# Keeping the first query gate's weights from the K projection on, with advance products of that gate alone

## The chip, the cores and the metric

The kernel runs as one program on one core of a Trainium2 chip. The metric is device time in microseconds (us). The engines are TensorE (PE: matmuls, with weight loads shown as PEld), VectorE (DVE), ScalarE (ACT), GpSimd (POOL) and SyncE (SP, which here only issues DMA transfers). Each engine works through its own queue in order; ACT's queue holds DMA issues too. SBUF is the on-chip memory, PSUM the memory into which PE adds up products.

## The reference

One layer of a transformer-like block over 1024 tokens of width 1024, in float32. What matters here is the first sub-layer:

```python
h = rmsnorm(x, ln1_g[l]) * (1.0 + sc1) + sh1
p = h @ w_in[l]
q, k, v, cb, cc, cx, ga, gb = jnp.split(p, split_at, axis=-1)
q = rmsnorm(q.reshape(b, s_len, SB_HEADS, SB_HEAD_DIM), q_norm_g[l])
k = rmsnorm(k.reshape(b, s_len, SB_HEADS, SB_HEAD_DIM), k_norm_g[l])
...
y_a = stick_breaking_attention(q, k, v)
y_b = cb * causal_dwconv(cc * cx, conv_w[l])
merged = (jax.nn.sigmoid(ga) * (y_a @ w_branch_a[l])
          + jax.nn.sigmoid(gb) * (y_b @ w_branch_b[l]))
x = x + g1 * (merged @ w_out[l])
```

After it come a second norm and a SwiGLU feed-forward part, which the change does not touch. All inputs are drawn at random; the norms' gains are scaled up (ln1_g by 2.738, q_norm_g and k_norm_g by 8).

## The kernel before

**Split numbers.** A float32 matrix is held as a high part and a low part (hi, lo), and a product is three matmuls: hi by hi, hi by lo, lo by hi. A weight tile `raw` (128 x 1024) comes from memory over SP. ACT writes its high part `whi` with a copy, and DVE the low part `wlo` with a subtraction. `g_split` (line 471) does so for half a tile, that is 128 x 512.

**Stages around the change.** The activations h are kept in SBUF, in four tiles named `big` (high and low part of two halves of the tokens). The K projection (from line 440) runs over two halves of the columns (`cc` 1 and 2) and eight blocks of 128 tokens (`i`); one block is 24 matmuls. Each block has a tail, `finish_k` (line 382): ACT squares the block (`qsq`), DVE sums per head (`qss`), POOL forms the reciprocal root (`rs_m`, `rs_r`), DVE scales (`qn`), PE transposes (four small matmuls into `tr`, line 396), ACT writes the high part `khl` (line 399), DVE its low part (line 400), and ACT issues two transfers to `d_k` (line 402). The transposes of a block come some blocks after it, so the last two stand behind the end of the projection.

While the K projection runs, a generator `factors` computes four combinations of the halves of h and writes them to memory as `d_t[6]`, `d_t[3]`, `d_t[5]`, `d_t[4]`, since SBUF has no room for them yet.

**The gates.** The other projections are computed as 20 "gates". Gate g makes two blocks of 128 output columns, j and j + 4, for all tokens. It is a Strassen-like scheme: the 2 x 2 blocks a11, a12 (tile `raw`) and a21, a22 (tile `raw2`) of the weights are combined on POOL to ws1 to ws4 (`s1` to `s4` in the code), and seven products are formed instead of eight. A product is 12 matmuls of 128 x 512 (`half_prod`, line 125) of one weight combination with one factor of h:

- p1: a11 with factor 0, and p2: a12 with factor 1; both factors lie in `big`
- p3: ws4 with factor 2, in `big` as well
- p4: a22 with factor 3, which is loaded from `d_t[3]` over a part of `big` that is free after the K projection (two transfers of 1 MB, line 632)
- p5: ws1 with factor 4, p6: ws2 with factor 5, p7: ws3 with factor 6; these are the tiles `ft`, of 2 MB each. `ft` 4 and 5 are loaded during the K projection (line 459), `ft` 6 after it (line 630), since its place is in a pool that opens only then

Gates 0 to 3 are the query gates (section 5, weights `w_q`). For them `put_q` writes q to memory and squares it, and `sum_q` adds up the squares with small matmuls (line 587) for the norm.

**Advance products.** Before the loop over gates, `first_two` loads `raw` of gates 0 and 1 and forms p1 and p2 of both (NG = 2): four products, in PSUM before the loop starts. Their loads and splits run during the K projection. In the loop, `two_raw` loads both weight tiles of a gate; it is called for gate g + 1 when POOL's work on gate g is issued. Two `raw` buffers exist (GR = 2). Gate 0's two tiles are loaded by a call of `two_raw(0)` ahead of the loop, so its `raw` is loaded twice, and gate 1's as well.

**Order.** The kernel is written in a tile language: a scheduler fixes each engine's order when the kernel is built, from the order of the program and a model of the time, and puts in the waits. `tc.issue_after(X)` keeps an instruction behind X in that order.

Of the kernel before, what the change touches and what calls it, by code (L numbers as in the profile page):

```python
# [8 lines left out]
F32 = mybir.dt.float32  # L9
F32R = mybir.dt.float32r  # L10
AF = mybir.ActivationFunctionType
ALU = mybir.AluOpType
# [4 lines left out]
P = 128  # L17
# [12 lines left out]
def block_kernel(tc, x, x_t, cols, ada_1, ada_2, ada_row, w_q, w_kv, w_v1, w_cg, w_a, w_b, w_o, w_g, w_u, w_d, out):  # L30
    nc = tc.nc
# [7 lines left out]
    def nm(s):  # L39
        uid[0] += 1  # L40
        return f"{s}_{uid[0]}"

    def big():
        return bigp.tile([P, KT, 512], F32R, tag="big", bufs=4, name=nm("big"))
# [9 lines left out]
    def load_w(src):  # L54

        wp, bufs = wps
        raw = gw.tile([P, 1024], F32, tag="raw", bufs=GR, name=nm("raw"))
        nc.sync.dma_start(raw, src)
        hi = wp.tile([P, 1024], F32R, tag="whi", bufs=bufs, name=nm("whi"))
        lo = wp.tile([P, 1024], F32R, tag="wlo", bufs=bufs, name=nm("wlo"))  # L60
        nc.scalar.activation(hi, raw, AF.Copy)
        nc.vector.tensor_tensor(out=lo, in0=raw, in1=hi.bitcast(F32), op=ALU.subtract)
        return hi, lo
# [15 lines left out]
    d_t = {q: drp.tile([P, 2, 4, 512], F32, name=f"d_t{q}") for q in (6, 3, 5, 4)}  # L79
# [46 lines left out]
    def half_prod(ps, w, fh, fl):  # L126

        wh = w[0].rearrange("p (k m) -> p k m", k=4)
        wl = w[1].rearrange("p (k m) -> p k m", k=4)
        for k in range(4):  # L130
            nc.tensor.matmul(ps, wh[:, k, :], fh[:, k, :], start=(k == 0), stop=False)  # L131
            nc.tensor.matmul(ps, wh[:, k, :], fl[:, k, :], start=False, stop=False)  # L132
            nc.tensor.matmul(ps, wl[:, k, :], fh[:, k, :], start=False, stop=(k == 3))  # L133

    def tt(eng, out, a, b, op):
        eng.tensor_tensor(out=out, in0=a, in1=b, op=op)  # L136
# [5 lines left out]
    def ps_pj():  # L142
        return pps.tile([P, 512], F32, tag="pj", bufs=6, name=nm("pj"))
# [6 lines left out]
    GR, NG, GS, GS2 = 2, 2, 4, 3  # L150
    gws = ExitStack()
    gw = gws.enter_context(tc.tile_pool(name="wpl", bufs=1, reuse_waits="tile"))
# [131 lines left out]
    def mm_tok(ps, i, w, k0, k1, parts=(0, 1, 2)):  # L284

        n, t0 = i // 4, (i % 4) * P
        for k in range(k0, k1):
            wh = w[k // 2][0][:, (k % 2) * 512:(k % 2) * 512 + 512]
            wl = w[k // 2][1][:, (k % 2) * 512:(k % 2) * 512 + 512]
            sh = hh[n][:, k, t0:t0 + P]  # L290
            sl = hl[n][:, k, t0:t0 + P]
            for q, (a, b) in enumerate(((sh, wh), (sh, wl), (sl, wh))):
                if q in parts:
                    nc.tensor.matmul(ps, a, b, start=(k == 0 and q == 0), stop=(k == KT - 1 and q == 2))  # L294
# [88 lines left out]
    def finish_k(ps, i, ch):  # L383
        sq = gw.tile([P, 512], F32, tag="wlo", bufs=GS, name=nm("qsq"))
        nc.scalar.activation(sq, ps, AF.Square)
        ss = ap.tile([P, 8], F32, tag="qss", bufs=3, name=nm("qss"))
        nc.vector.tensor_reduce(out=ss, in_=sq.rearrange("p (h d) -> p h d", d=DH), op=ALU.add, axis=AX.X)
        qn = ap.tile([P, 512], F32, tag="qn", bufs=2, name=nm("qn"))
        r = rstd_of(ss, 1.0 / DH, ap, 8)
        nc.vector.tensor_tensor(out=qn.rearrange("p (h d) -> p h d", d=DH),  # L390
                                in0=ps.rearrange("p (h d) -> p h d", d=DH),
                                in1=r.unsqueeze(2).broadcast_to([P, 8, DH]), op=ALU.mult)
        yield
        tr = ps_tr()
        for j in range(4):
            nc.tensor.transpose(tr[:, j * P:(j + 1) * P], qn[:, j * P:(j + 1) * P], ident)
        hl_ = ap.tile([P, 2, 512], F32R, tag="vs", bufs=4, name=nm("khl"))
        hi, lo = hl_[:, 0], hl_[:, 1]
        nc.scalar.activation(hi, tr, AF.Identity, scale=kgc)
        nc.vector.scalar_tensor_tensor(out=lo, in0=tr, scalar=kgc, in1=hi.bitcast(F32), op0=ALU.mult, op1=ALU.subtract)  # L400
        for e, t in ((0, hi), (1, lo)):
            nc.scalar.dma_start(d_k[e][4 * ch:4 * ch + 4, :, i * P:(i + 1) * P].rearrange("j p t -> p j t"),
                                t.rearrange("p (j t) -> p j t", j=4).bitcast(F32))
# [9 lines left out]
    tails = []  # L413
# [19 lines left out]
    def more():  # L433

        with tc.issue_after(ends[0]), tc.issue_after(ends[1]):
            next(ml, None)

    for cc in (1, 2):
        w = wq[4:] if cc == 1 else [load_w(w_kv[cc, j]) for j in range(4)]
        for i in range(8):  # L440
            ps = ps_pj()
            mm_tok(ps, i, w, 0, 8)
            while len(tails) >= 2:
                next(tails.pop(0), None)
            tails.append(finish_k(ps, i, cc - 1))
            next(tails[-1])
            for _ in range(2 if (cc, i) < (1, 4) else 3):
                more()
            if (cc, i) == (2, 1):
                for _ in ml:  # L450
                    pass
                s2b.close()
                sx.close()
# [3 lines left out]
    ft = {q: ftp.tile([P, 2, 4, 512], F32R, name=f"ft{q}") for q in (5, 4)}  # L457
# [3 lines left out]
    def g_bank():  # L461
        return ps_pj()

    def g_raw(src):
        raw = gw.tile([P, 1024], F32, tag="raw", bufs=GR, name=nm("raw"))
        last_raw[0] = nc.sync.dma_start(raw, src)
        return raw

    last_raw = [None]

    split_at = [gw]

    def g_split(src):
        split_at.append(split_at.pop(0))
        hi, lo = (split_at[0].tile([P, 512], F32R, tag=t_, bufs=GS if split_at[0] is gw else GS2, name=nm(t_))
                  for t_ in ("whi", "wlo"))
        nc.scalar.activation(hi, src, AF.Copy)  # L477
        tt(nc.vector, lo, src, hi.bitcast(F32), ALU.subtract)
        return hi, lo

    fac = {0: (hh[0][:, 0:4], hl[0][:, 0:4]), 1: (hh[0][:, 4:8], hl[0][:, 4:8]), 2: (hh[1][:, 4:8], hl[1][:, 4:8])}
    def g_prod(w, q):
        ps = g_bank()
        half_prod(ps, w, *fac[q])
        return ps

    gates = ([(5, j) for j in range(4)] + [(sec, j) for j in range(4) for sec in (1, 2)] +
             [(sec, j) for sec in (4, 3) for j in range(4)])

    def w_of(sec, m):  # L490
        return w_q[m] if sec == 5 else w_cg[sec, m]

    pre = {}

    def first_two(g):
        sec, j = gates[g]
        raw = g_raw(w_of(sec, j))
        return g_prod(g_split(raw[:, :512]), 0), g_prod(g_split(raw[:, 512:]), 1)

    for g in range(NG):  # L500
        pre[g] = first_two(g)
        if g == 0:
            for tl in tails:
                next(tl, None)

    def two_raw(g):
        sec, j = gates[g]
        return g_raw(w_of(sec, j)), g_raw(w_of(sec, j + 4))

    s2.close()  # L510
    sw.close()
# [78 lines left out]
    def end_q():  # L590

        ss = [g_tile()[:H] for n in range(2)]
        for n in range(2):
            nc.scalar.activation(ss[n], ssq[n], AF.Copy)
        yield
        tr = g_bank()
        for i in range(8):
            nc.tensor.transpose(tr[:, i * H:(i + 1) * H], ss[i // 4][:, i % 4 * P:(i % 4 + 1) * P], ident[:H, :H])
        ms = gp.tile([P, 8, H], F32, name="ms16")
        nc.vector.tensor_scalar(out=ms.rearrange("p i h -> p (i h)"), in0=tr[:, :8 * H], scalar1=1.0 / DH, scalar2=EPS,  # L600
                                op0=ALU.mult, op1=ALU.add)
        for i in range(8):
            for h in range(0, H, 8):
                yield
                nc.gpsimd.tensor_tensor(out=rq[:, 0, i, h:h + 8], in0=ms[:, i, h:h + 8], in1=nhalf, op=ALU.pow)
        nc.vector.tensor_scalar(out=rq[:, 1], in0=rq[:, 0], scalar1=-1.0, scalar2=None, op0=ALU.mult)
# [18 lines left out]
        nc.scalar.dma_start(d_y[m, :, s:s + 512], y)  # L625

    uc = {}
    raws = two_raw(0)
    pend, pmm, eq = [], [], end_q()
    nc.sync.dma_start(ft[6].bitcast(F32), d_t[6])  # L630
    for e in range(2):
        nc.sync.dma_start(fac[3][e].bitcast(F32), d_t[3][:, e])
    for g, (sec, j) in enumerate(gates):
        raw, raw2 = raws
        p1, p2 = pre[g] if g in pre else (g_prod(g_split(raw[:, :512]), 0), g_prod(g_split(raw[:, 512:]), 1))
# [6 lines left out]
        if g + 1 < len(gates):  # L642
            raws = two_raw(g + 1)
# [374 lines left out]
    for n in range(2):  # L1018
        for k in range(KT):
            yr = fp.tile([P, 512], F32, tag="yr", bufs=2, name=nm("yr"))  # L1020
            nc.sync.dma_start(yr, d_ya[n][:, k, :])
            tag, bufs = slots[n * KT + k]
# [134 lines left out]
    tails, pre = [], {}  # L1157
    for ch in range(2):
        w = [] if ch else list(w_pre)
        for j in range(len(w) // 2, 4):  # L1160
            raw = load_raw(w_o[ch, j])
# [89 lines left out]
    th, tl = big(), big()  # L1251
# [335 lines left out]
```

## Time and profile before

| what | us |
|---|---|
| median of 3 runs | 1845.73 |
| lowest and highest run | 1843.6, 1846.24 |
| the profiled execution, its own time | 1843.09 |
| span of the profiled execution | 1841.3 |
| mean granted PE clock, share of full speed | 0.997 |

The page gives the busy time of each engine, the chain of work that ended last, and groups of instructions. A row of the view in order of time reads: start, length (of a merged group), engine, line, operation, the tile written and the tiles read, and in brackets the idle time before it and what ended it. In a row of the windows view come the length, then for PE, PEld, DVE, ACT and POOL the busy time with the number of instructions, then the granted PE clock, the share of time for which the DMA engines were busy, and GB/s. The view of waits gives who waited for whom: total, times, longest. A matmul's shown length reaches past the start of the next, so its cost is the distance of starts.

### The profile page before, as it was taken

To read this page: it belongs to the slowest core of one execution; us is meant where nothing else is said; L and a number is where in the kernel's file an instruction comes from. 1 tells how busy PE (TensorE), PEld (TensorE's weight loads), DVE (VectorE), ACT (ScalarE), POOL (GpSimd) and SP (SyncE) were. 2 spreads that over 40 slices of the span, in tenths; PEclk is the share of its full clock that TensorE was granted. 3 is DMA by queue.
4 is the path that set the end of the run, shared out by engine and by line. 5 is a ranking of instruction groups with operands and counts; after the bars stand their busy time and mean duration, and the time that the engine had idled before them with its cause. 6 is when DMAs were issued, how large, how long until landed. Compare 5 with 4: busy or idle time off the path is not lost.

```text
span 1841.3 us, 24885 instructions
## 1 busy us (share of the span) xinstructions
PE 1804.7 (98%) x8829; PEld 1502.7 (82%) x8829; DVE 1350.0 (73%) x1948; ACT 792.0 (43%) x1494; POOL 370.3 (20%) x277
## 2 busy tenths in 40 slices
PE   7999999999999999999999999999999999999999
PEld 4787778888879988888888788877888888878887
DVE  6874776779874888888887644589977788644776
ACT  4352553333343656565665311663444344422321
POOL 1043327423240000000000000105543454200000
PEclk9999999999999999999999999999999999999999
DMA  9588452227748565678554635424533344299766
GB/s 394 192 318 291 166 189 86 81 75 253 277 162 253 152 193 172 186 230 272 158 141 136 208 126 206 138 93 159 206 137 142 133 172 172 103 335 339 280 231 220
DMA packets 147267, 358.01 MB, mean 194 GB/s; under 512 B 15480, under 2 KB 44480, under 8 KB 144968
## 3 DMA queue, kind: packets, MB, share of 16 engines
q1 hardware_dynamic: 101816, 289.12, 46.2%
q10 hardware_dynamic: 44320, 63.64, 9.9%
q0 software_dynamic: 1008, 3.67, 0.5%
q8 instruction: 70, 1.15, 0.3%
q14 instruction: 53, 0.43, 0.1%
HBM read 245.74 MB, written 110.66 MB: 194 GB/s over the span
## 4 chain that ended last, share of the span: by engine, by line
PE 73%; DVE 11%; DMA 9%; ACT 3%; issue 3%; POOL 1%; SPq 0%; ACTq 0%; DVEq 0%; POOLq 0%
PE e L132 6%; PE e L131 6%; PE e L133 6%; PE pj L131 5%; PE pj L133 5%; PE pj L132 5%; PE pj L294 5%; PE pj L880 4%; PE pj L881 4%; PE pj L882 4%; PE e L1414 3%; PE e L1416 3%; PE e L1415 3%; PE tr L807 3%; PE o L823 2%
## 5 line engine op out<-in xcount | busy, mean ns | idle before, releaser
L792 DVE TENSOR_TENSOR_SCAN pt<-pt,mk 128x128 f32<-128x128 f32 (+7 forms) x128 | 171.9, 1349 | 47.3 <-ACT pt L788 47.1
L788 ACT ACTIVATE pt<-z,rq 128x512 f32<-128x512 f32 (+3 forms) x192 | 107.1, 579 | 89.5 <-PE z L787 57.6
L131 PE MATMUL e<-big,whi 128*128 128x512 f32 x352 | 137.2, 390 | 2.2 <-ACT c L1314 2.2
L133 PE MATMUL e<-big,wlo 128*128 128x512 f32 x352 | 137.1, 389 | 0.0
L132 PE MATMUL e<-big,whi 128*128 128x512 f32 x352 | 137.0, 389 | 0.0
L122 POOL TENSOR_SCALAR rs_m<-ss 128x1 f32<-128x1 f32 x8 | 1.7, 211 | 653.7 <-ACT xn L1217 653.7
L136 DVE TENSOR_TENSOR c<-e,c 128x512 f32<-128x512 f32 x138 | 92.8, 686 | 54.6 <-PE e L133 53.7
L131 PE MATMUL pj<-big,whi 128*128 128x512 f32 x320 | 125.1, 391 | 0.8 <-DVE c L136 0.8
L132 PE MATMUL pj<-big,whi 128*128 128x512 f32 x320 | 124.7, 390 | 0.0
L133 PE MATMUL pj<-big,wlo 128*128 128x512 f32 x320 | 124.3, 390 | 0.0
L1414 PE MATMUL e<-whi,f 128*128 128x512 f32 (+1 forms) x319 | 121.7, 382 | 1.6 <-DMA f<-d_f 1.6
L1415 PE MATMUL e<-wlo,f 128*128 128x512 f32 (+1 forms) x319 | 121.8, 382 | 0.0
L1416 PE MATMUL e<-whi,f 128*128 128x512 f32 (+1 forms) x319 | 121.6, 382 | 0.0
L294 PE MATMUL pj<-whi,big 128*128 128x512 f32 x352 | 110.0, 398 | 4.0 <-ACT big L277 3.9
L136 DVE TENSOR_TENSOR wlo<-raw,whi 128x512 fp32r<-128x512 f32 x116 | 88.4, 766 | 33.9 <-ACT whi L477 33.8
L136 DVE TENSOR_TENSOR c<-pj,c 128x512 f32<-128x512 f32 x140 | 93.1, 681 | 27.5 <-PE pj L133 26.9
L136 POOL TENSOR_TENSOR ws<-raw,raw 128x512 f32<-128x512 f32 x40 | 57.2, 1429 | 273.6 <-DMA raw<-w_cg 129.0
L477 ACT ACTIVATE whi<-raw 128x512 fp32r<-128x512 f32 x116 | 72.6, 629 | 88.3 <-PE pj L132 37.7
L811 DVE TENSOR_TENSOR atl<-tr,ath 128x512 fp32r<-128x512 f32 (+1 forms) x192 | 99.5, 547 | 14.4 <-ACT ath L810 12.6
L132 PE MATMUL e<-rl,whi 128*128 128x512 f32 x264 | 103.5, 392 | 2.5 <-DVE rl L136 2.5
L810 ACT ACTIVATE ath<-tr 128x512 fp32r<-128x512 f32 (+1 forms) x192 | 86.8, 489 | 44.5 <-PE o L822 26.0
L807 PE MATMUL tr<-dm,pt 128*128 128x128 f32 x576 | 98.0, 274 | 6.2 <-DVE atl L811 5.6
(255 smaller groups left out, 5021.6 us busy)
## 6 DMA issues: line engine op xcount, KB each, us to landing
f<-d_f SPq DMA_DIRECT2D x77, 512.0 KB, 4.3
d_f<-fs SPq DMA_DIRECT2D x70, 512.0 KB, 3.2
raw<-w_cg SPq DMA_DIRECT2D x40, 512.0 KB, 4.3
raw<-w_u SPq DMA_DIRECT2D x26, 512.0 KB, 3.2
raw<-w_g SPq DMA_DIRECT2D x25, 512.0 KB, 3.5
ad<-ada ACTq DMA_DIRECT2D x19, 512.0 KB, 5.5
ada<-ada SPq DMA_DIRECT2D x8, 1024.0 KB, 9.9
d_t<-ts SPq DMA_DIRECT2D x16, 512.0 KB, 4.0
```

The costliest lines, as they stand in the source:

```text
L131: nc.tensor.matmul(ps, wh[:, k, :], fh[:, k, :], start=(k == 0), stop=False)
L132: nc.tensor.matmul(ps, wh[:, k, :], fl[:, k, :], start=False, stop=False)
L133: nc.tensor.matmul(ps, wl[:, k, :], fh[:, k, :], start=False, stop=(k == 3))
L136: eng.tensor_tensor(out=out, in0=a, in1=b, op=op)
L294: nc.tensor.matmul(ps, a, b, start=(k == 0 and q == 0), stop=(k == KT - 1 and q == 2))
L788: nc.scalar.activation(pt[:, off + s0:off + s0 + m], z[:, :m], AF.Sigmoid, scale=rq[:, 1, i, h:h + 1])
L792: nc.vector.tensor_tensor_scan(out=pt[:, rev], data0=pt[:, rev], data1=mk[:, rev], initial=1.0, op0=ALU.mult, op1=ALU.max)
L807: nc.tensor.transpose(tr[:, j * P:(j + 1) * P], pt[:, off + (b0 + j) * P:off + (b0 + j + 1) * P], ident)
L811: nc.vector.tensor_tensor(out=tl[:, :nb, c0:c0 + P], in0=src, in1=th[:, :nb, c0:c0 + P].bitcast(F32), op=ALU.subtract)
L1414: nc.tensor.matmul(o, sh, w[0][:, c], start=(j == 0), stop=False)
L1415: nc.tensor.matmul(o, sh, w[1][:, c], start=False, stop=False)
L1416: nc.tensor.matmul(o, sl, w[0][:, c], start=False, stop=(j == NJ - 1))
```

## The change

The weights of gate 0 (`raw` and `raw2`) are loaded in the K projection, at block 3 of its second half, into the two `raw` buffers, and stay there until the loop uses them. The two halves of `raw` are split at that place. After the projection p1 and p2 of gate 0 alone are formed in advance; gate 1's come in the loop, as for the later gates. The call `two_raw(0)` ahead of the loop is gone, and with it the second load of gate 0's `raw` and the separate load of gate 1's: two loads of 512 KB fewer. The loads of `ft` 6 and of the two halves of factor 3 are held behind gate 0's second weight load, and in this order behind each other. The functions `g_raw`, `g_split`, `w_of`, `two_raw` and the list `gates` move up unchanged.

```diff
     for cc in (1, 2):
         w = wq[4:] if cc == 1 else [load_w(w_kv[cc, j]) for j in range(4)]
         for i in range(8):
+            if (cc, i) == (2, 3):
+                raws = two_raw(0)
+                pre_w = g_split(raws[0][:, :512]), g_split(raws[0][:, 512:])
             ps = ps_pj()
             mm_tok(ps, i, w, 0, 8)
...
-    pre = {}
-
-    def first_two(g):
-        sec, j = gates[g]
-        raw = g_raw(w_of(sec, j))
-        return g_prod(g_split(raw[:, :512]), 0), g_prod(g_split(raw[:, 512:]), 1)
-
-    for g in range(NG):
-        pre[g] = first_two(g)
-        if g == 0:
-            for tl in tails:
-                next(tl, None)
...
+    pre = {0: (g_prod(pre_w[0], 0), g_prod(pre_w[1], 1))}
+    for tl in tails:
+        next(tl, None)
...
     uc = {}
-    raws = two_raw(0)
     pend, pmm, eq = [], [], end_q()
-    nc.sync.dma_start(ft[6].bitcast(F32), d_t[6])
+    with tc.issue_after(last_raw[0].ins):
+        ld = nc.sync.dma_start(ft[6].bitcast(F32), d_t[6])
     for e in range(2):
-        nc.sync.dma_start(fac[3][e].bitcast(F32), d_t[3][:, e])
+        with tc.issue_after(ld.ins):
+            ld = nc.sync.dma_start(fac[3][e].bitcast(F32), d_t[3][:, e])
     for g, (sec, j) in enumerate(gates):
         raw, raw2 = raws
```

More of the change, by code (lines that the diff above doesn't have):

```diff
@@ L436, in more, with g_raw, g_split, w_of @@
             next(ml, None)
+    def g_raw(src):
+        raw = gw.tile([P, 1024], F32, tag="raw", bufs=GR, name=nm("raw"))
+        last_raw[0] = nc.sync.dma_start(raw, src)
+        return raw
+    last_raw = [None]
+    split_at = [gw]
+    def g_split(src):
+        split_at.append(split_at.pop(0))
+        hi, lo = (split_at[0].tile([P, 512], F32R, tag=t_, bufs=GS if split_at[0] is gw else GS2, name=nm(t_))
+                  for t_ in ("whi", "wlo"))
+        nc.scalar.activation(hi, src, AF.Copy)
+        tt(nc.vector, lo, src, hi.bitcast(F32), ALU.subtract)
+        return hi, lo
+    gates = ([(5, j) for j in range(4)] + [(sec, j) for j in range(4) for sec in (1, 2)] +
+             [(sec, j) for sec in (4, 3) for j in range(4)])
+    def w_of(sec, m):
+        return w_q[m] if sec == 5 else w_cg[sec, m]
+    def two_raw(g):
+        sec, j = gates[g]
+        return g_raw(w_of(sec, j)), g_raw(w_of(sec, j + 4))
     for cc in (1, 2):
@@ L462, in g_bank @@
         return ps_pj()
[L464 to L479, printed above, removed]
     fac = {0: (hh[0][:, 0:4], hl[0][:, 0:4]), 1: (hh[0][:, 4:8], hl[0][:, 4:8]), 2: (hh[1][:, 4:8], hl[1][:, 4:8])}
@@ L485, in g_prod @@
         return ps
[L487 to L491, printed above, removed]
-    pre = {}
-    def first_two(g):
-        sec, j = gates[g]
-        raw = g_raw(w_of(sec, j))
-        return g_prod(g_split(raw[:, :512]), 0), g_prod(g_split(raw[:, 512:]), 1)
-    for g in range(NG):
-        pre[g] = first_two(g)
-        if g == 0:
-            for tl in tails:
-                next(tl, None)
-    def two_raw(g):
-        sec, j = gates[g]
-        return g_raw(w_of(sec, j)), g_raw(w_of(sec, j + 4))
+    pre = {0: (g_prod(pre_w[0], 0), g_prod(pre_w[1], 1))}
+    for tl in tails:
+        next(tl, None)
     s2.close()
```

## The prediction

> **What bounds the kernel now.** I read the page first: its share of busy time and the chain that ended last.
>
> ```profile
> span 1841.3 us, 24885 instructions
> PE 1804.7 (98%) x8829; PEld 1502.7 (82%) x8829; DVE 1350.0 (73%) x1948; ACT 792.0 (43%) x1494; POOL 370.3 (20%) x277
> PE 73%; DVE 11%; DMA 9%; ACT 3%; issue 3%; POOL 1%; SPq 0%; ACTq 0%; DVEq 0%; POOLq 0%
> ```
>
> TensorE (PE) is busy 98% of the span, so whatever does not open or close a gap on PE is worth nothing here. All 24 moved matmuls stay in the program, so the question is only which PE gaps lie where the change acts: between the end of the K projection and the third gate. Second view: who PE waited for between 80 and 300 us.
>
> ```profile
> PE pj L131 <- ACT whi L477: 2.3, 1, 2.3
> PE tr L587 <- ACT gt L579: 0.7, 1, 0.7
> PE tr L587 <- DVE gt L136: 0.3, 1, 0.3
> ```
>
> These three are all that can be won by closing waits: 2.3 + 0.7 + 0.3 = 3.3 us. The first is the join between the advance products and the loop over gates. The other two are sums for the q norm that wait for a square and its split. Third view: PE in order of time around that join.
>
> ```profile
> 166.88 0.48 PE L131 MATMUL pj<-big,whi 128*128 128x512 f32 x1
> ...
> 168.82 0.60 PE L396 MATMUL tr<-dm,qn 128*128 128x128 f32 x4
> 169.17 0.48 PE L133 MATMUL pj<-big,wlo 128*128 128x512 f32 x1
> ...
> 178.63 0.40 PE L133 MATMUL pj<-big,wlo 128*128 128x512 f32 x1
> 181.29 0.80 PE L131 MATMUL pj<-ft,whi 128*128 128x512 f32 x1 [2.27 <-ACT whi L477]
> 181.88 0.63 PE L132 MATMUL pj<-ft,whi 128*128 128x512 f32 x1
> ...
> 191.09 0.39 PE L131 MATMUL pj<-big,whi 128*128 128x512 f32 x1
> ...
> 196.31 0.39 PE L133 MATMUL pj<-big,wlo 128*128 128x512 f32 x1
> ```
>
> 166.88 is the first advance product. From 191.09 to 196.31 stand 24 matmuls, so one takes (196.31 - 191.09) / 23 = 0.227 us, and a product of 12 takes 2.72. A group of four transposes takes 169.17 - 168.82 = 0.35. After the gap, matmuls last 0.63 instead of 0.39. The windows view shows what that is:
>
> ```profile
> 181.30:184.70 3.40, 3.40 (x8) 2.70 (x9) 3.36 (x5) 1.49 (x3) 0.41 (x1) 0.52 0.93 286
> 1271.70:1275.10 3.40, 3.40 (x15) 2.80 (x16) 3.37 (x6) 2.02 (x4) 0.00 (x0) 1.00 1.04 405
> ```
>
> The third number from the end is the granted PE clock: 0.52 for the 3.4 us after this gap, in which 8 matmuls run. The same length at clock 1.00 holds 15. So the low clock costs another 7 x 0.227 = 1.6 us. The gap counted from matmul starts is 181.29 - 178.63 - 0.23 = 2.43.
>
> **The change part by part.** *Two loads fewer.* Before, the weights of the first query gate are fetched once for the advance products and again for the loop. Now both halves are fetched at the two places in SP's order where the two advance loads stood, and kept. 1 MB of traffic and two issues go. No PE wait named a load of these, so I take 0 for it. The lower bound is a gain of one landing, if it alone held the join:
>
> ```profile
> raw<-w_q SPq DMA_DIRECT2D x10, 512.0 KB, 5.2
> ```
>
> *Splits.* Four advance splits become two, and the second gate's two go into the loop, each on ACT and DVE: the same number of instructions on each engine. *SP's order.* The reload of gate 0 stood ahead of the 2 MB load ft6; now ft6 and the two 1 MB halves of factor 3 come first, then the second gate's weights. In the built kernel the order of instructions differs from that of before only between the second half of the K projection and the third gate (three pairs of DVE instructions aside, much later). After that all engines run the same order, so what is lost or won here is carried unchanged to the end.
>
> *The gap, the main term.* The 24 products of gate 1 leave the place where they covered ACT's work after the K projection. In the new PE order both last transpose groups stand behind the 24 products that are left: PE is through at 166.88 + 24 x 0.227 + 2 x 0.35 = 173.0. Then it waits for the split of ws2 on ACT, as before. What ACT does between the transposes and that split:
>
> ```profile
> 167.93 0.37 ACTq L402 DMA_DIRECT2D d_k<-khl  x1
> 169.45 0.69 ACT L399 ACTIVATE khl<-tr,cst 128x512 fp32r<-128x512 f32 x1 [1.56 <-PE tr L396]
> ...
> 177.92 1.15 ACTq L402 DMA_DIRECT2D d_k<-khl  x2
> 179.12 1.08 ACT L670 ACTIVATE c<-pj 128x512 f32<-128x512 f32 x2 [1.23 <-DVE uu L613]
> 180.09 1.67 ACT L477 ACTIVATE whi<-ws 128x512 fp32r<-128x512 f32 x3
> ```
> ```profile
> 177.92 0.75 DVE L400 SCALAR_TENSOR_TENSOR khl<-tr,cst,khl 128x512 fp32r<-128x512 f32 x1 [6.40 <-ACT khl L399]
> ```
>
> New ACT order: khl, khl, four d_k issues, one copy of c, split of ws1, split of ws2. A khl starts 169.45 - 168.82 = 0.63 after its transposes. The first group begins at 166.88 + 5.45 = 172.33, so khl starts at 172.96 and the second 0.64 later, ending at 174.29. The last d_k issue needs DVE's low part of the second, two DVE instructions of 0.75 after 173.65, so 175.15; with 0.37 for the issue, 175.5. One copy: 0.49 (half of 180.09 - 179.12), 176.0. Two splits at 1.67 / 3 = 0.56: PE starts at **177.1**. Applied to before, where one khl starts at 177.20 and two copies follow, the same steps give 181.2 against the 181.29 shown. The new gap is 177.1 - 173.0 = 4.1, against 2.43: **+1.7 us**. POOL is the other limit:
>
> ```profile
> 168.41 1.64 POOL L123 TENSOR_TENSOR rs_r<-rs_m,nhalf 128x8 f32<-128x8 f32 x1
> 176.61 1.28 POOL L136 TENSOR_TENSOR ws<-raw,raw 128x512 f32<-128x512 f32 x1 [6.57 <-DMA raw<-w_q]
> 177.85 1.28 POOL L136 TENSOR_TENSOR ws<-raw 128x512 f32<-128x512 f32 x1
> 179.10 1.26 POOL L136 TENSOR_TENSOR ws<-raw,ws 128x512 f32<-128x512 f32 x1
> ```
>
> Before, POOL waited 6.57 us for the reloaded weights. Now they are there, and ws1 and ws2 follow the last rs_r: 170.05 + 3 x 1.26 = 173.8. That wait is truly removed, but ACT's queue in front of the split ends later. If ACT's queue did not hold it, PE would start at 173.8 + 0.6 = 174.4, a gap of 1.4. Bounds of this term: from -1.0 (POOL's gap) to +1.7; I take ACT's, since it is in order and each step has its row.
>
> *The clock.* Two gaps of this kernel were not followed by a low clock:
>
> ```profile
> 1271.68 0.50 PE L131 MATMUL e<-big,whi 128*128 128x512 f32 x1 [2.18 <-ACT c L1314]
> ```
> ```profile
> 1627.24 0.47 PE L1414 MATMUL e<-whi,f 128*128 128x512 f32 x1 [1.64 <-DMA f<-d_f]
> ```
>
> A gap of 2.27 was, a gap of 2.18 was not. A gap of 4.1 is longer than any of these, so I take one low stretch, 1.6 us, in both kernels: 0. Bounds -1.6 and +1.6 (none, or two stretches).
> The Trainium skill (TensorE: Matmul & The Clock Gate, Part 1: The HAM clock gate) says that PE falls to half rate after an idle window of about 3.4 us and is released after a busy window of that length. The trace agrees with the length and rate of the low stretch, and not with the idle time, 2.27 us here. By that rule the old gap would cost no clock and the new one would, which is a rival below.
>
> *The sums for the q norm.* Their waits of 0.7 and 0.3 came when gate 1 began with its third product. Now two more products (5.4 us) stand ahead, and the sums among them. I take -0.8 of the 1.1, bounds 0 and -1.1.
>
> *Gate 1's loads, now on the path.* Its first product begins at 177.1 + 60 x 0.227 + 1.6 = 192.3. What comes before it on SP, and how long transfers took (transfers by kind with their median to landing; SP in order of time; whom SP's issue of ft6 waited for; landings of raw, then of d_k, shortest, median and longest; two windows with the share of the DMA engines second to last):
>
> ```profile
> ft<-d_t SPq DMA_DIRECT2D x3, 2048.0 KB, 8.8
> ...
> d_k<-khl ACTq DMA_DIRECT2D x32, 256.0 KB, 4.4
> big<-d_t SPq DMA_DIRECT2D x2, 1024.0 KB
> ```
> ```profile
> 175.52 0.33 SPq L630 DMA_DIRECT2D ft<-d_t  x1
> ```
> ```profile
> SPq L630 <- DMA d_k<-khl: 5.8, 1, 5.8
> ```
> ```profile
> DMA to landing us min/median/max: 3.2/4.2/10.2
> ```
> ```profile
> DMA to landing us min/median/max: 2.2/4.4/14.9
> ```
> ```profile
> 170.00:175.00 5.00, 5.00 (x24) 4.11 (x23) 1.35 (x2) 0.14 (x1) 0.04 (x1) 1.00 1.00 316
> 175.00:180.00 5.00, 4.02 (x20) 3.00 (x18) 0.77 (x3) 1.57 (x3) 3.39 (x3) 1.00 1.12 369
> ```
>
> ft6 now needs only the end of the K projection (166.6): with 8.8 it lands at 175.4 and is used at 177.1 + 24 x 0.227 + 1.6 = 184.2. In the built kernel the second half of factor 3 waits for the d_k landing that released ft6 at 175.52; with at most 8.8 it is there at 184.3, used at 189.6. Gate 1's first weights wait for the next d_k landing, about 177, and with 10.2 (the longest of a weight load) land at 187.2; with 1.3 for the split that leaves 3.8 us. The second need the split of gate 0's last quarter (ACT and DVE, to about 180.5), land by 190.7, and with POOL's 3.8 and a split are ready at 195.1 for PE's 197.8. All are covered by gate 0's 60 matmuls, so I take 0; the DMA engines are full (1.00, 1.12) in this stretch, so the upper bound is the second rival.
>
> **Sum.** 0 + 1.7 + 0 - 0.8 + 0 = +0.9 us. The profiled execution took 1843.09 us, 1.8 around its span of 1841.3, so it would take 1844.0. The median of the three runs, 1845.73, is 2.64 above it; I put the 0.9 on the median: **1846.6 us**.
>
> **The rivals.** *The join closes.* PE does not wait for ACT's queue: the gap is POOL's 1.4 (-1.0) or none (-2.4), without low clock (-1.6) and without the sums' waits (-0.8 to -1.1). That is -3.4 to -5.1, 1842.3 to 1840.6; I price it at 1841.5. For it speaks POOL's 6.57 us wait, which goes; against it, the four d_k issues and two khl that stand ahead of the split on ACT.
> *The clock.* The old gap usually costs no low clock and the new one always does: +1.7 + 1.6 - 0.8 = +2.5, 1848.2. For it, the 2.18 us gap at clock 1.00; against it, the 0.52 after 2.27. This is what the Trainium skill's rule (TensorE: Matmul & The Clock Gate, Part 1) would make of it.
> *Gate 1's weights land late* (the other side). PE, which before had gate 1's first two products done, stands at their start. It decides from a landing later than 191 for the first or 193 for the second load. If the latter takes 14.9 us, as the slowest d_k transfer did, it lands at 195.4, ws2's split is ready at 199.7, and PE stands 1.9 us, with 1.6 of low clock: 0.9 + 3.5 = +4.4, 1850.1. For it, full DMA engines and 4 MB queued ahead; against it, several us of slack at each step.
> *The change does nothing*: gap, clock and sums as before, 1845.7.
>
> **How the numbers follow.** Forecast 0.48, clock 0.12, does nothing 0.05, late weights 0.17, join closes 0.18. A difference of 0.2% is 3.7 us, about what a measurement of this kernel can tell from no change. Late weights are over it and so is most of the closed join (0.16 of 0.18, with 0.02 short of it); of the forecast I give 0.03 to slower and 0.01 to faster, for errors in the terms. Slower 0.20, faster 0.17, same 0.48 + 0.12 + 0.05 + 0.02 - 0.04 = 0.63. The range goes from 1841.8, inside the closed join, to 1850.4, just over the late weights.
>
> **What would show it.** Right: PE waits once at the join, 4 us, for ACT's whi; POOL's first ws follows rs_r without a DMA wait; khl twice, then four d_k issues, on ACT before it; 8 matmuls of 0.63 behind it; no wait of L587's successor above 0.3; gate 1's first product without a wait. Wrong: a gap under 2.5 us at the join (ACT's queue mis-timed), a PE wait for raw or ft in gates 0 to 2 (loads), or a time off by over 4 us with this stretch as forecast, which would put the cause where the order is unchanged.

## The result and the profile after

The changed kernel takes 1852.34 us (median of 7 runs, 1849.2 to 1857.84) where the kernel before takes 1843.6 in the same comparison (7 runs, 1839.81 to 1846.24): ratio 1.0041, 95% interval 1.0029 to 1.0053. By this ratio it is slower by about 7.6 us (the medians differ by 8.7). I had forecast 0.9 us more than before; my 1846.6 and its range up to 1850.4 were too low. The profiled execution took 1849.2 us; its page says:

```profile
span 1847.4 us, 24886 instructions
...
PE 1804.0 (98%) x8829; PEld 1504.5 (81%) x8829; DVE 1349.1 (73%) x1948; ACT 794.1 (43%) x1494; POOL 368.3 (20%) x277
...
PE 80%; DVE 10%; DMA 4%; issue 2%; ACT 2%; ACTq 0%; SPq 0%; POOL 0%; DVEq 0%; POOLq 0%
```

PE is as busy as before (1804.0 against 1804.7 us), so the 6.1 us that the span grew are time in which PE stood. Whom it waited for between 80 and 300 us is now one line (total, times, longest):

```profile
PE pj L131 <- ACT whi L451: 9.0, 1, 9.0
```

The two waits of the sums for the q norm are gone, and the wait at the join has grown from 2.3 to 9.0 us. PE in order of time at that place:

```profile
172.32 1.03 PE L396 MATMUL tr<-dm,qn 128*128 128x128 f32 x8
182.36 0.80 PE L131 MATMUL pj<-ft,whi 128*128 128x512 f32 x1 [9.01 <-ACT whi L451]
182.96 0.63 PE L132 MATMUL pj<-ft,whi 128*128 128x512 f32 x1
```

Both groups of transposes stand behind the 24 advance products, as forecast, and PE is free where I had it (172.32 + 2 x 0.35 = 173.0). But the first matmul of the next product comes at 182.36, not at 177.1. ACT in order of time shows what it did until then:

```profile
172.96 1.26 ACT L399 ACTIVATE khl<-tr,cst 128x512 fp32r<-128x512 f32 x2 [5.20 <-PE tr L396]
173.68 6.95 ACTq L402 DMA_DIRECT2D d_k<-khl  x4
180.67 0.60 ACT L665 ACTIVATE c<-pj 128x512 f32<-128x512 f32 x1 [6.45 <-issue]
181.17 1.66 ACT L451 ACTIVATE whi<-ws 128x512 fp32r<-128x512 f32 x3
```

This is the forecast order, khl, khl, four d_k issues, c, splits, and the khl start at the forecast 172.96. Yet the four issues, for which I had reckoned until 175.5, last until 180.63. The chain of waits (start, length, engine or queue, line) has them one by one:

```profile
174.25 2.08 ACTq L402
...
176.37 3.27 ACTq L402
...
179.68 0.94 ACTq L402
```

The first of the four took the usual 0.37, the other three 2.08, 3.27 and 0.94. From 174.25 on ACT computes nothing: it stands in the issue of a transfer, and the copy c and the splits that PE needs are queued behind. POOL had long been ready, right after its last rs_r and without a wait for weights:

```profile
169.88 1.30 POOL L136 TENSOR_TENSOR ws<-raw,raw 128x512 f32<-128x512 f32 x1
...
172.38 1.27 POOL L136 TENSOR_TENSOR ws<-raw,ws 128x512 f32<-128x512 f32 x1
```

What changed for the transfers is seen in SP's queue. After, in order of time:

```profile
166.58 0.32 SPq L624 DMA_DIRECT2D ft<-d_t  x1
166.95 13.95 SPq L627 DMA_DIRECT2D big<-d_t  x2
```

The second row merges two issues of 0.3 to 0.4 us each (shortest, median, longest in ns, start of the first and of the last):

```profile
L627 SPq DMA_DIRECT2D big<-d_t x2: 319/371/423, 167.0 to 180.6; - x2
```

And before, a row that I had passed over:

```profile
163.77 0.80 SPq L632 DMA_DIRECT2D big<-d_t  x2
```

Before, factor 3 (`big`, 2 x 1 MB) was fetched from 163.77 on, that is while the K projection still ran and not after it, and ft6 (2 MB) from 175.52. The change chains factor 3 behind ft6: ft6 goes out 9 us earlier and factor 3 later. Its first half follows at 166.95. These 3 MB now move up to 179.6, across the time in which ACT has to issue the last d_k writes (by the trace's DMA packets, 0.9 MB are left at the first of these). The second half of factor 3 goes out at 180.6, when the d_k issues are over.

How much of the 6.1 us lies here? I take the starts of the 600th and the 1200th matmul (154 and 293 us before: ahead of the join, and several gates behind it). Between them lie 139.63 us before and 144.47 after: **4.8 us**. Taken as distances of matmul starts over 0.23 each, this is the gap at the join with 9.05 against 2.44 (+6.6), the two waits for the sums, 0.5 and 0.9, which are gone (-1.4), the low stretch with 1.4 against 1.6 (-0.2), and another -0.2. The order of instructions behind is the same in both kernels. From the 1200th to the 1700th matmul all eleven profiles of this study take 113.3 us. The four stretches from there to the end (starts at 407, 543, 810 and 1195 us before) differ by 1.9 to 6.1 us among the eleven, and between the two runs of the changed kernel (this one and c1) by up to 1.6. The other 1.3 us of the two profiles lie there, and I don't explain them.

### The profile page after: what moved, and what is told of

Its sections match the earlier page's. It is cut to its first block, busy times and chain, and to the rows that moved or that the text cites. A ratio compares the mean times of both kernels' runs of the same rounds, so it can differ in the third digit from the quotient of the medians.

```text
span 1847.4 us, 24886 instructions
## 1 busy us (share of the span) xinstructions
PE 1804.0 (98%) x8829; PEld 1504.5 (81%) x8829; DVE 1349.1 (73%) x1948; ACT 794.1 (43%) x1494; POOL 368.3 (20%) x277
## 3 DMA queue, kind: packets, MB, share of 16 engines
q8 instruction: 70, 1.15, 0.3%
## 4 chain that ended last, share of the span: by engine, by line
PE 80%; DVE 10%; DMA 4%; issue 2%; ACT 2%; ACTq 0%; SPq 0%; POOL 0%; DVEq 0%; POOLq 0%
PE e L131 7%; PE e L132 7%; PE e L133 7%; PE pj L131 6%; PE pj L133 6%; PE pj L132 6%; PE pj L294 5%; PE pj L875 4%; PE e L1409 4%; PE e L1411 4%; PE e L1410 4%; PE pj L876 4%; PE pj L877 4%; PE tr L802 3%; PE o L818 2%
```

## The experiments

Theory (held issues): the d_k issues on ACT stand because data that was queued earlier is still moving, and everything behind them on ACT, and PE, stands with them. Rivals: one unlucky execution; ACT's queue is simply this long; the loads slow PE itself. Where a kernel was timed, the ratio is to the kernel before on the same chip.

**c1: the changed kernel once more**, with no edit.

> The changed kernel once more, as the control of this group. Its profile had a PE gap of 9.0 us at the join, of which ACT's four d_k issues took 6.95 us. Theory (held issues: the d_k issues on ACT stand while the 4 MB of factor loads fill the DMA engines): gap 8 to 10 us again, four issues 6 to 8 us, 7 to 9 us slower than before. Rival (one unlucky execution; the ordinary gap is the 4.1 us of ACT's short rows): gap 4 to 5 us here, issues under 2.5 us.

Ratio 1.0032 (1.0023 to 1.0042). PE waits 8.7 us at the join, and ACT in order of time shows the same picture:

```profile
173.78 6.67 ACTq L402 DMA_DIRECT2D d_k<-khl  x4
```

Not one unlucky execution.

**e1: both factor loads behind gate 1's first weights**, in gate 0, so that they are issued when ACT is past its d_k issues.

```diff
-    with tc.issue_after(last_raw[0].ins):
-        ld = nc.sync.dma_start(ft[6].bitcast(F32), d_t[6])
-    for e in range(2):
-        with tc.issue_after(ld.ins):
-            ld = nc.sync.dma_start(fac[3][e].bitcast(F32), d_t[3][:, e])
...
+        if g == 0:
+            n_sec, n_j = gates[1]
+            r1 = g_raw(w_of(n_sec, n_j))
+            with tc.issue_after(last_raw[0].ins):
+                ld = nc.sync.dma_start(ft[6].bitcast(F32), d_t[6])
...
+            with tc.issue_after(ld.ins):
+                raws = r1, g_raw(w_of(n_sec, n_j + 4))
```

> The same, with the loads of ft6 and of factor 3 behind the second gate's first weight load, so that they are issued at about 175 us, after the d_k issues. Held issues: the four d_k issues take under 2.5 us, the gap at the join is 4 to 5 us, and the time falls by 4 to 6 us against the changed kernel, unless factor 3 comes late for the fifth product (a PE wait for it, up to 4 us, would then eat it). Rival (the queue in front of the split is long by itself, the loads have no part): gap 9 us as in the changed kernel, no gain.

Ratio 1.0001 (0.999 to 1.0012). ACT, then SP, in order of time:

```profile
173.86 2.20 ACTq L402 DMA_DIRECT2D d_k<-khl  x4
176.11 0.60 ACT L670 ACTIVATE c<-pj 128x512 f32<-128x512 f32 x1 [1.70 <-DVE uu L607]
```
```profile
175.18 0.33 SPq L440 DMA_DIRECT2D raw<-w_q  x1
175.68 0.42 SPq L636 DMA_DIRECT2D ft<-d_t  x1
```

Nothing but the place of three loads in SP's order was changed, and the loss is gone. The four issues take 2.20 us, PE's only wait is 4.3 us at the join, and the time is that of before: the kernel that my prediction describes.

**e4: no factor loads at all.** The products p4 and p7 use factors 2 and 5 instead, and the later restoring of `big` is left out, so these products are not the reference's.

```diff
-    fac[3] = (hh[1][:, 0:4], hl[1][:, 0:4])
+    fac[3] = fac[2]
+    fac[6] = fac[5]
...
-    with tc.issue_after(last_raw[0].ins):
-        ld = nc.sync.dma_start(ft[6].bitcast(F32), d_t[6])
-    for e in range(2):
-        with tc.issue_after(ld.ins):
-            ld = nc.sync.dma_start(fac[3][e].bitcast(F32), d_t[3][:, e])
```

> The changed kernel without the loads of ft6 and of the two halves of factor 3 and without the two loads that restore that part of big after the gates; the products p7 and p4 use factors 5 and 2 in their place, so this part of the output differs. Held issues: the four d_k issues take 1.5 to 2 us, gap 4.1 us, no later PE wait, and the time falls by 5 to 6 us against the changed kernel, to about that of before. Rival (queue long by itself): gap 9 us.

Ratio 1.0002 (0.999 to 1.0014), PE's only wait 4.3 us, and on ACT in order of time:

```profile
173.74 2.21 ACTq L402 DMA_DIRECT2D d_k<-khl  x4
```

So 2.2 us is what these four issues take with nothing in their way; that is also the bound of what moving loads can win here.

**e2: the last two blocks' d_k transfers issued by SP.**

```diff
-            nc.scalar.dma_start(d_k[e][4 * ch:4 * ch + 4, :, i * P:(i + 1) * P].rearrange("j p t -> p j t"),
+            (nc.sync if ch == 1 and i > 5 else nc.scalar).dma_start(
+                d_k[e][4 * ch:4 * ch + 4, :, i * P:(i + 1) * P].rearrange("j p t -> p j t"),
```

> The changed kernel with the d_k issues of the last two K blocks on SP in place of ACT. Held issues: ACT goes from the second khl straight to the copy of c and the two splits; PE starts at 174.3 + 0.5 + 1.1 = 175.9, the gap is about 2.9 us, 6 us less than in the changed kernel; SP's own queue is held, so the factor loads and the second gate's weights come later and may bring a new PE wait in gates 0 or 1. Rival (queue long by itself): the four issues are worth their 1.5 us at most, gap 7 us or more.

Ratio 1.0028 (1.0015 to 1.0041). Whom PE waited for between 80 and 300 us, and SP in order of time:

```profile
PE pj L131 <- ACT whi L452: 2.4, 1, 2.4
PE pj L131 <- DMA ft<-d_t: 2.2, 1, 2.2
PE tr L582 <- DVE gt L136: 1.2, 2, 1.0
PE tr L582 <- ACT gt L574: 0.9, 1, 0.9
```
```profile
174.00 2.19 SPq L402 DMA_DIRECT2D d_k<-khl  x4
176.30 0.52 SPq L625 DMA_DIRECT2D ft<-d_t  x1
```

The wait at the join falls to 2.4, near the gap of 2.9 expected from an ACT without these issues. But SP, in order too, now holds ft6 back until the d_k issues are done, and PE waits for ft6 and for the sums instead. The expectation had left such waits open; they take the win back, since the issues were moved to another queue with work behind them.

**f1 and f2: one of the two factors early, the other behind gate 1's first weights.** f1 leaves ft6 where the change put it and moves factor 3:

```diff
-    for e in range(2):
-        with tc.issue_after(ld.ins):
-            ld = nc.sync.dma_start(fac[3][e].bitcast(F32), d_t[3][:, e])
...
+        if g == 0:
...
+            r1 = g_raw(w_of(n_sec, n_j))
+            ld = last_raw[0]
+            for e in range(2):
+                with tc.issue_after(ld.ins):
+                    ld = nc.sync.dma_start(fac[3][e].bitcast(F32), d_t[3][:, e])
```

f2 moves ft6, and factor 3 follows gate 0's second weight load directly:

```diff
-    with tc.issue_after(last_raw[0].ins):
-        ld = nc.sync.dma_start(ft[6].bitcast(F32), d_t[6])
+    ld = last_raw[0]
...
+            with tc.issue_after(last_raw[0].ins):
+                ld = nc.sync.dma_start(ft[6].bitcast(F32), d_t[6])
```

> As the changed kernel, but the two halves of factor 3 (2 MB) are issued in gate 0 behind the first weight load of gate 1; only ft6 (2 MB) stays early, at about 166.6. Held issues (T): what holds the last four d_k issues is the amount of data that is queued ahead of them. With 2 MB instead of 3 to 4 MB ahead, and 7 us (166.6 to 173.7) to move it, most of ft6 has passed when they come: the four issues take 2.2 to 4.5 us (6.95 with both loads, 2.21 with none), the join's gap is 4.3 to 6.5 us, the time 0 to 3 us above the kernel before (ratio 1.000 to 1.0015). Rival (one load is the cause by itself, here ft6): the issues take 6 to 7 us as in the changed kernel, gap near 9, ratio 1.003 to 1.004.

> The counterpart: the two halves of factor 3 stay early (both issued at about 166.6, 2 MB), ft6 (2 MB) is issued in gate 0 behind the first weight load of gate 1. T (amount of data ahead): the four d_k issues take 2.2 to 4.5 us, gap 4.3 to 6.5 us, ratio 1.000 to 1.0015, as with ft6 alone early. Rival (one load is the cause by itself, here factor 3): 6 to 7 us for the issues, gap near 9, ratio 1.003 to 1.004. ft6 is used by the third product behind the join and may be waited for if it comes after 184.

f1: ratio 1.0025 (1.0014 to 1.0037), PE's wait 6.2 us. f2: ratio 1.0001 (0.9989 to 1.0013), waits 4.3 us at the join and 0.9 for ft6. ACT of f1 in order of time, then ACT, SP and a window of f2 (share of the DMA engines second to last):

```profile
174.91 4.15 ACTq L402 DMA_DIRECT2D d_k<-khl  x4
```
```profile
173.76 2.21 ACTq L402 DMA_DIRECT2D d_k<-khl  x4
```
```profile
163.72 0.80 SPq L626 DMA_DIRECT2D big<-d_t  x2
```
```profile
172.00:174.00 2.00, 1.44 (x11) 1.07 (x9) 0.24 (x1) 0.96 (x2) 1.92 (x3) 1.00 0.11 34
```

With ft6 alone early (2 MB) the issues take 4.15 us, between 2.2 (no loads) and 6.95 (3 MB), which speaks for the amount queued. The time of f1 came out above what I expected (at most 1.0015); it has three low-clock windows (176.7 to 187.0 us), of which the first falls into the wait and PE runs in the other two, where the kernel before has one. In f2 my premise was wrong in a useful way. Without the chain behind ft6, factor 3 goes out at 163.72, as before the change, and is through when the d_k issues come: the DMA engines are 0.11 busy from 172 to 174, and the issues take 2.21. Not the size of a load decides, but whether it is over by then.

**f3, f4, f5: a version without the join.** POOL forms gate 0's combinations between its rs_r of the K projection's last blocks, ACT splits ws2 there, POOL issues the last two blocks' d_k transfers, and SP's order is changed. The core of the edit:

```diff
+            if cc == 2 and i in (5, 6):
+                next(ahead)
...
+    def combine_ahead():
...
+            tt(nc.gpsimd, s3, a11, a21, ALU.subtract)
+            tt(nc.gpsimd, s2_, a22, s3, ALU.subtract)
...
-            nc.scalar.dma_start(d_k[e][4 * ch:4 * ch + 4, :, i * P:(i + 1) * P].rearrange("j p t -> p j t"),
+            (nc.gpsimd if ch == 1 and i > 5 else nc.scalar).dma_start(
...
-        p6 = g_prod(g_split(s2_), 5)
+        p6 = g_prod(w_0[6] if g == 0 else g_split(s2_), 5)
```

> A version made to beat both. POOL forms gate 0's weight combinations in its idle time during the K projection and ACT splits ws2 there, so that PE has a product to run at the join without waiting for ACT; the last two blocks' d_k transfers are issued by POOL, which has nothing urgent then; the order of SP is ft6, gate 1's first weights, factor 3, gate 1's second weights. T: with no d_k issues ahead of ACT's splits the early loads cost PE nothing: no gap over 1 us between 165 and 182, no low clock there, so 2.4 + 1.6 us less than the kernel before, and the waits of 0.7 and 0.3 in gate 1 go: 1840 to 1843 where the kernel before takes 1846.6 (ratio 0.997 to 0.9985). What may take a part back: ft6 lands at 175.4 at the earliest and is needed at 178.4, a sum for the norm now stands ahead of the third product, and factor 3 is needed at 184. Rival (the loads slow PE itself, through operand reads or shared memory, and not ACT's issues): PE still loses 4 to 5 us between 166 and 190, in gaps or longer matmuls, and the ratio stays above 1.002.

A miss: ratio 1.0041 (1.0029 to 1.0054). The join is closed up to a wait of 0.8 us for a split on ACT. PE then waits 11.3 us for a split on DVE. DVE in order of time:

```profile
187.69 0.09 DVE L643 MEMSET uu<- 128x2 f32 x2 [10.89 <-DMA d_k<-khl]
```

By this wait, tile `uu` had come to lie where a K block was still on its way to d_k, and DVE's whole queue stood until that write had landed. Here not the issue but the landing was late (up to 18.9 us after the issue), and it hit another engine.

**f4** takes that clearing out of the way (behind gate 3), gate 0's splits use buffers that hold no K block, and ws1 is split ahead too; factor 3 goes out in the idle DMA time, then ft6, then gate 1's weights.

```diff
-            for e in range(2):
-                nc.vector.memset(uu[e][:, :2], 0.0)
+            for e in range(2):
+                with tc.issue_after(last_ws4[0].ins):
+                    nc.vector.memset(uu[e][:, :2], 0.0)
...
+    w_0[5] = g_split(w_0["ws"][0])
...
-    with tc.issue_after(last_raw[0].ins):
-        ld = nc.sync.dma_start(ft[6].bitcast(F32), d_t[6])
+    ld = last_raw[0]
     for e in range(2):
         with tc.issue_after(ld.ins):
             ld = nc.sync.dma_start(fac[3][e].bitcast(F32), d_t[3][:, e])
+    with tc.issue_after(ld.ins):
+        ld = nc.sync.dma_start(ft[6].bitcast(F32), d_t[6])
```

> The closed join again, without the new wait of f3: there DVE stood 10.9 us at the clearing of two small tiles whose memory had held a K block that was still on its way to d_k. Now that clearing comes after gate 3; gate 0's splits take their buffers from the other pool, ws1 is split ahead too; the two halves of factor 3 are issued in the idle DMA time at 163.7 (as in f2), then ft6, then gate 1's weights; the last two blocks' d_k transfers stay with POOL. T (held issues and late landings hurt only through what is queued behind them on an engine): no PE wait over 1 us between 165 and 182 and no low clock there, so about 4 us less than the kernel before: 1840 to 1843 where that takes 1845 to 1846, ratio 0.997 to 0.999. ft6 should land at 177 to 178.5 for its use at 178.4; a wait of up to 1.5 us there is possible. Rival (the loads themselves slow PE): gaps or longer matmuls of 4 to 5 us remain between 166 and 190, and the ratio is not below 1.000.

Ratio 0.9975 (0.9962 to 0.9989), 1841.05 us (12 runs). PE and POOL in order of time, and whom PE waited for from 160 to 300 us:

```profile
173.47 0.60 PE L398 MATMUL tr<-dm,qn 128*128 128x128 f32 x4
173.82 0.48 PE L133 MATMUL pj<-ft,whi 128*128 128x512 f32 x1
```
```profile
175.09 1.74 POOL L404 DMA_DIRECT2D d_k<-khl  x2 [4.04 <-ACT khl L401]
177.38 1.54 POOL L404 DMA_DIRECT2D d_k<-khl  x2 [0.54 <-ACT khl L401]
```
```profile
PE tr L618 <- ACT gt L610: 2.8, 1, 2.8
PE tr L618 <- DVE gt L138: 0.3, 1, 0.3
```

PE goes from the transposes into the next product without a wait, while 4 MB of loads move beside it. Its matmuls start 0.23 us apart, as elsewhere, with the DMA engines 1.00 busy from 174 to 176. So the loads do not slow PE itself here; they hurt through what is queued behind held issues and late landings. One new wait of 2.8 us is left, a sum for the q norm that the scheduler put into the middle of gate 0.

**f5** holds these sums behind the last product that stands before them in the program.

```diff
+            with tc.issue_after(last_mm[0].ins):
+                nc.tensor.matmul(ssq[n], sel[:, 14 - 2 * m:30 - 2 * m], t, start=(nss[n] == 0), stop=(nss[n] == 15))
```

> As f4, with the sums for the q norm held behind the last product that stands before them in the program, since in f4 PE stood 2.8 us at the first of them (in the middle of gate 0, for a square on ACT) and ran on at half clock after it. T: that wait and its low clock go (2.8 + about 1.3), unless ft6, which is used right there, is late by up to 1.5 us: ratio to the kernel before 0.995 to 0.9975 (f4: 0.9975). Rival (the sum only covered a wait for ft6, since the loads are at their limit there): PE waits for ft6 at the same place by 1.5 to 3 us, and the ratio stays at 0.997 to 0.998.

Ratio 0.9962 (0.9951 to 0.9974), 1837.76 us (12 runs): it beats both kernels. ft6 was not waited for and the wait in gate 0 is gone, but a wait of 2.7 us, again for a sum's square, stands in gate 1 now; the wait was moved, not removed:

```profile
PE tr L621 <- ACT gt L612: 2.7, 1, 2.7
```

By the starts of the 600th and 1200th matmul, this version needs 138.37 us and f4 138.69, against 139.63 before. That is 1 us, not the 3.5 and 7.4 between the medians. Another 0.7 to 1.1 us lie in the stretch from 407 to 543 us (135.67 and 136.11 against 136.78), where these versions' splits use other buffers; the rest I can't place. f3 to f5 change several things at once, and their gain over the kernel before is not divided among them.

| kernel | four d_k issues | PE's wait at the join | matmul 600 to 1200 | ratio to before |
|---|---|---|---|---|
| before | 1.15 (two of them) | 2.3 | 139.63 | 1 |
| after | 6.95 | 9.0 | 144.47 | 1.0041 |
| c1, after again | 6.67 | 8.7 | 145.45 | 1.0032 |
| f1, ft6 early | 4.15 | 6.2 | 143.19 | 1.0025 |
| e1, both loads later | 2.20 | 4.3 | 140.97 | 1.0001 |
| f2, factor 3 at 163.72 | 2.21 | 4.3 (and 0.9) | 141.01 | 1.0001 |
| e4, no loads | 2.21 | 4.3 | 139.98 | 1.0002 |

## Why the prediction was wrong

**The step that failed** is in the gap, the main term: "The last d_k issue needs DVE's low part of the second [...] so 175.15; with 0.37 for the issue, 175.5." The mechanism was right (PE waits for ACT's queue: khl, khl, four issues, c, splits). Mis-sized were the issues: 0.37, 2.08, 3.27 and 0.94 us, ending at 180.63. Reckoned as there, the gap became 182.36 - 173.0 = 9.3 instead of 4.1, that is 5.2 us more than the term had. c1, f1, f2, e1 and e4 show what sets it: 6.7 to 7.0 us with 3 MB of loads ahead, 4.15 with ft6 alone, 2.2 with none ahead or with loads that are through.

**The step behind it** is "SP's order". I wrote that "now ft6 and the two 1 MB halves of factor 3 come first", and took its effect to be nothing but landing times, which all had slack. The row at 163.77 shows that factor 3 had come first all along, in idle DMA time, and that the change delays it. And I asked of each moved load who waits for it, not what it would do to the transfers issued beside it. The kernel before would have told me. ACT's d_k pairs there while ft4 and ft5 moved and just after, in order of time; SP's issue of these; the landing of a transfer of the first pair; and the issues of the second pair (shortest, median, longest, ns):

```profile
138.25 1.82 ACTq L402 DMA_DIRECT2D d_k<-khl  x2
...
144.18 4.11 ACTq L402 DMA_DIRECT2D d_k<-khl  x2
...
150.12 3.12 ACTq L402 DMA_DIRECT2D d_k<-khl  x2
...
156.06 1.17 ACTq L402 DMA_DIRECT2D d_k<-khl  x2
```
```profile
137.14 1.59 SPq L459 DMA_DIRECT2D ft<-d_t  x2
```
```profile
DMA to landing us min/median/max: 14.9/14.9/14.9
```
```profile
L402 ACTq DMA_DIRECT2D d_k<-khl x2: 367/1837/3307, 144.2 to 145.0; - x2
```

4 MB of loads, and the next three pairs take 1.82, 4.11 and 3.12 us instead of 1.17. There ACT had slack and nobody waited. I had quoted the 14.9 as a landing time, and not asked what an issue does while its predecessors don't land.

The other steps, one by one:

- *Two loads fewer, splits, POOL*: right. No PE wait names a weight load, and POOL's first ws follows rs_r at 169.88 without a DMA wait (forecast end 173.8, it was 173.7).
- *PE free at 173.0, khl at 172.96*: right.
- *The undisturbed gap of 4.1*: a little more where loads don't disturb (e4: 177.68 - 173.1 = 4.6, with a wait of 4.3, as in e1 and f2), because even then the issues end at 176.0 and not at 175.5.
- *The sums*: right in kind, larger in size. Both waits are gone, -1.4 by distances of matmul starts instead of -0.8.
- *The clock*: one stretch of cost in both, as taken. In the changed kernel's two low windows, which begin at 178.42, PE stands in the first and runs 7 matmuls in the second. In c1 and f1 it was a window more, so this term varies by one window with the execution.
- *Gate 1's loads late* (the rival that I gave the other side): wrong as a mechanism, no wait for them. Its price of 1850.1 was the nearest of the four to the result, by chance.
- *The join closes*: did not happen in the changed kernel, but f4 shows the condition for it: ACT's d_k issues and the splits out of the way.

As for the bounds: I had set the gap's upper bound at my own estimate (+1.7), since each step "has its row". But the row that I took (0.37 at 167.93) was of an issue with nothing of its own queue left to move. The three right behind it, from 169.51, which my lines leave out, took 0.37, 0.44 and 0.67 there. The longest of the kernel before, 3.31 us, is 2.9 above it; for the three issues behind the first that bounds the term at +1.7 + 8.8, and the measured +6.9 lies inside.

## What to carry to other kernels

A transfer that is issued earlier is not only ready earlier: it takes the DMA engines from whatever is issued beside it, and an engine that issues a write then may stand in the issue, with its computation queued behind. So look at the durations of the issue instructions on engines that also compute, in a stretch where large loads move, before a load is moved there; and look up where each load really stands in the order, not in the program. Put large loads where the DMA engines are idle and nobody is about to issue (f2), or issue the writes from an engine without urgent work (f4), and check what is queued behind them there (e2, f3).

## What the runs showed of the hardware

**An issue is engine time, and its length is not fixed.** The d_k issue on ACT took 0.37 us undisturbed and up to 3.27 at the join. The Trainium skill (DMA: Bandwidth & Descriptors, Issuing engines are not separate DMA queues) says that issuing from several engines saves only the time on the sequencer, "which is usually small relative to the DMA itself"; here that time decided, and the measurement goes before. The Trainium skill (Perfetto Trace Analysis, DMA Instruction — HWDGE) says that the time shown for an issue holds a wait for the descriptor generator and the generation, not the movement of the data. Rows from 0.37 to 3.27 fit that, but no row here shows these parts apart.

**What the long issues have in common is their own queue's backlog.** Loads in flight are not enough: before, the pair at 177.92 took 1.15 us with ft6 moving since 175.52. They are not needed at that moment either: before, the issue at 150.92 took 2.32 us while SP's queue moved 0.03 MB. The DMA packets in the traces show how much of ACT's earlier d_k writes (512 packets each) had not yet started to move when an issue began. Of the 336 d_k issues on ACT in the eleven profiles, 87 found fewer than 60 packets waiting, and all took 0.37 to 0.41 us, 53 of them while SP's queue moved over 0.2 MB per us. The 22 that took over 1.41 us all found 1450 or more, near three writes or beyond (150.92: 1701; the two long ones at the join: 1451 and 1905). It is no threshold, since 8 others with as many took 0.37. So the loads seem to act by holding up ACT's earlier writes; no run changed the backlog alone, and what exactly fills up stays open.

**The same wait is followed by a low clock or not.** In f1 and f2 PE waited 2.09 us at the same instruction; PE in order of time and the window from there (f1, granted clock third from the end), then the same of f2:

```profile
523.15 0.50 PE L133 MATMUL pj<-ft,wlo 128*128 128x512 f32 x1 [2.09 <-DVE wlo L136]
```
```profile
523.15:526.56 3.41, 3.41 (x15) 2.84 (x16) 3.41 (x7) 1.95 (x4) 0.00 (x0) 1.00 0.78 258
```
```profile
519.37 0.79 PE L133 MATMUL pj<-ft,wlo 128*128 128x512 f32 x1 [2.09 <-DVE wlo L136]
```
```profile
518.74:522.15 3.41, 2.78 (x7) 2.20 (x8) 3.41 (x7) 1.25 (x3) 0.00 (x0) 0.50 0.84 275
```

15 matmuls at full clock in one, 7 at half clock in the other. So a wait near 2 us has no fixed price, and my reading of 2.18 and 2.27 us as the two sides of a limit was wrong. The Trainium skill (TensorE: Matmul & The Clock Gate, Part 1) says that the window over which PE's activity is judged runs freely. That agrees: in each of the eleven traces the low windows begin whole steps of 3.413 us apart (before, 181.12 and 1235.84 are 309 steps apart), wherever PE's waits lie. Its idle window of about 3.4 us does not agree, since a wait of 2.09 us sufficed here.
